# HGRN2 sample states updated by VectorE and ScalarE in half-head steps, without the GpSimd passes

## The chip, the cores and the metric

The kernel runs on one core of one Trainium2 chip, in one launch. The metric is the device time of that core in microseconds (us). Three runs of the kernel before took 1523.41, 1524.83 and 1525.97 us; the median, 1524.83 us, is the time before.

## The reference, cut to what matters

One step of a hybrid decoder layer works on 256 prompt tokens and 8 sample tokens (one new token for each of 8 running sequences). A projection of width 88 x 128 feeds a short convolution and an HGRN2 recurrence with 8 heads of 128 x 128 state; their outputs are merged by gates, projected, and followed by a squared-ReLU MLP. For a sample token the recurrence is one step of the state, and its output is a product with q:

```python
f = lb + (1.0 - lb) * sigmoid(fz)
kk = 1.0 - f
S = f[..., None] * S + kk[..., None] * v[None, :]     # per sequence and head, 128 x 128
o = q @ S
```

All sample states of the 8 heads (8 x 8 x 128 x 128 float32, 4 MB) are read, updated and written back.

## The kernel before, in words

Features lie on partitions, the 264 tokens on the free axis. Every matrix product is formed from exact halves: an operand x is split into `hi` (a rounded copy, ScalarE, line 58) and `lo` (x minus `hi`, VectorE, line 59), and each 128 x 128 weight block takes three matmuls (lines 85 to 87). So each weight chunk of 128 x 2048 (1 MB, one output tile of 128 features) asks for two casts `whi` on ScalarE, two subtractions `wlo` on VectorE, both 1024 columns wide, and 48 matmuls on TensorE.

The input projection (phase 1) is written out by hand as a list of 56 slots, `seq`. In slot i the program issues, in this order: the fetch of the weights of tile i + 2 (SyncE's queue), the evacuation of tile i - 1 from PSUM (VectorE, line 445), the casts and subtractions for tile i + 1, the work that stands in `todo` for the slot, then the 48 matmuls of tile i, then the TensorE work in `todo_pe`. Two raw weight buffers and four `whi`/`wlo` buffers (two tiles) connect the engines. Each engine works through its own queue strictly in order.

The recurrence of two heads (2j and 2j + 1) is cut into stages 0 to 14, one for each successive slot (function `hgrn`; the last lines of it list them). The stages that matter here:

- Stage 3 issues six transfers of 512 KB: for each head `so` (the state), `fb` and `qb` (f and q of the sample tokens, broadcast to all partitions).
- Stage 4: VectorE multiplies `kend`, `kin`, `qin`; GpSimd runs `s_mul(0)`: `so = so * fb`, then `fb = 1 - fb` (lines 254, 255). TensorE transposes `iv` and `kend` after the slot's matmuls (lines 298, 299).
- Stage 5: ScalarE copies `vk` (line 305); GpSimd runs `s_mul(1)`; VectorE runs `s_upd(0)`: eight times `so[:, t] = fb[:, t] * v + so[:, t]` on 128 columns (line 260). TensorE runs `sco(0)` (lines 314, 320).
- Stage 6: VectorE runs `sta(0)` (lines 325 to 329), which empties the PSUM tiles of `sco(0)`; there are three such tiles, so `sco(1)`, at the end of the slot, waits for `sta(0)`.
- Stage 7: `sta(1)`; GpSimd runs `s_out(0)`: `qb = qb * so` (line 265), and `so` is sent out. TensorE runs `ops` (lines 343, 347).
- Stages 8 to 10: `s_upd(1)`, then `s_red(0)` (a sum of `qb`, line 269) and `s_out(1)`, then `s_red(1)`.

Pair 0 has stage 4 in slot 8; pair 1 in slot 20, pair 2 in slot 32, pair 3 in slot 44. The convolution's work lies between: `conv_u` on GpSimd, `conv` one slot later (ScalarE line 409, then VectorE line 411), `conv_split` one slot after that.

Of the kernel before, what the change touches and what calls it, by code (L numbers as in the profile page):

```python
# [11 lines left out]
AF = mybir.ActivationFunctionType  # L12
ALU = mybir.AluOpType
# [3 lines left out]
TP = 256  # L17
TS = 8
# [20 lines left out]
@with_exitstack  # L39
def hybrid_step(ctx: ExitStack, tc: tile.TileContext, x, par, sconv, shg, w_hd, w_in, w_br, w_out, w_up, w_dn,  # L40
                y, nconv_p, nhg_p, nconv_s, nhg_s):
    """Feature-major throughout: features on partitions, the 256 prompt and 8 sample tokens on the free
    axis.  Every GEMM operand is split exactly into float32r parts (hi + lo), and each product is formed
    as hi*hi + hi*lo + lo*hi in float32 PSUM."""
    nc = tc.nc
    PS = bass.MemoryType.PSUM

# [20 lines left out]
        return w  # L68

    def split_w(w, h):  # L70
        """Half h of a [128, 16*128] weight chunk -> list of 8 (hi, lo) stationary tiles."""
        hi = wsp.tile([P, 8, P], F32R, tag="hi", name="whi")
        lo = wsp.tile([P, 8, P], F32R, tag="lo", name="wlo")
        split(w[:, h * 1024:(h + 1) * 1024].rearrange("p (k c) -> p k c", c=P), hi, lo)
        return [(hi[:, k], lo[:, k]) for k in range(8)]
# [16 lines left out]
    def t264(name):  # L92
        return tmp.tile([P, T], F32, tag="t", name=name)

# [1 line left out]
    ones = const.tile([P, P], F32, name="ones")  # L96
    nc.vector.memset(ones, 1.0)
    eps = const.tile([P, 1], F32, name="eps")
    nc.vector.memset(eps, EPS)
    warm = const.tile([P, 1], F32, name="warm")  # L100
# [5 lines left out]
    NB = T // 3  # L106

    def sumsq(ps, ss, start, stop):
        """Column sums of ss, tokens on partitions: ps[t, b] = sum over p of ss[p, b * NB + t]."""
        for b in range(3):  # L110
            nc.tensor.matmul(ps[:NB, b:b + 1], ss[:, b * NB:(b + 1) * NB], ones[:, 0:1],
                             start=(start and b == 0), stop=(stop and b == 2))

    def rstd_diag(ps, n, name):
        """Diagonal blocks of 1/sqrt(sum/n + eps) from the column sums in ps."""
        r = const.tile([NB, 3], F32, name="r_" + name)
        nc.vector.tensor_scalar(r, ps[:NB, 0:3], 1.0 / n, EPS, op0=ALU.mult, op1=ALU.add)
        nc.vector.reciprocal(r, r)
        nc.scalar.activation(r, r, AF.Sqrt)
        dg = const.tile([NB, 3, NB], F32, tag="dg", name="dg_" + name)  # L120
        nc.vector.tensor_tensor(dg, ident[:NB, 0:NB].unsqueeze(1).broadcast_to([NB, 3, NB]),
                                r.unsqueeze(2).broadcast_to([NB, 3, NB]), op=ALU.mult)
        return dg

    def rstd_bcast(dg, name):
        """The per-token factors of dg, on all partitions, in PSUM."""
        bps = mps.tile([P, 512], F32, tag="m", name="bps_" + name)[:, :T]
        nc.tensor.matmul(bps, ones[:NB], dg.rearrange("p b t -> p (b t)"), start=True, stop=True)
        return bps

# [1 line left out]
    pt = const.tile([P, N_PAR], F32, name="pt")  # L132
    xg = []
    ss1 = const.tile([P, T], F32, name="ss1")
# [4 lines left out]
    for g in range(4):  # L139
# [9 lines left out]
        for j in range(4):  # L149
            k = 4 * g + j  # L150
            gk = pt[:, C_NMIX + k:C_NMIX + k + 1]
            hi = act.tile([P, T], F32R, tag="xg", name=f"xgh{k}")
# [17 lines left out]
    nc.gpsimd.tensor_tensor(ss1, xsq[:, 0], xsq[:, 1], op=ALU.add)  # L170
    p0.close()

# [1 line left out]
    ident = const.tile([P, P], F32, name="ident")  # L174
    make_identity(nc, ident)
    cmask = const.tile([P, 2, P], F32, name="cmask")
# [5 lines left out]
    nc.gpsimd.memset(smask, 1.0)  # L182
    nc.gpsimd.memset(smask.rearrange("p a (n l) -> p (a n) l", l=CH)[:, :, 0:1], 0.0)

# [1 line left out]
    rstd1 = const.tile([P, T], F32, name="rstd1")  # L186
    ao = {}
    hctx = ExitStack()
# [15 lines left out]
        nc.gpsimd.memset(u[:, 0:2], 0.0)  # L204

    def hgrn(j, q, fz, iv, og):
        """HGRN2 of heads 2j, 2j+1, cut into stages that are issued beside successive GEMM tiles:
        stage -> (elementwise part, TensorE part)."""
        st = {}

        def s0():
# [37 lines left out]
                                    b3[:, :, CH - 1:CH].broadcast_to([P, 8, CH]), b3, op=ALU.subtract)  # L249
            st["b"] = b.rearrange("p (a t) -> p a t", a=2)  # L250

        def s_mul(i):
            fb, qb, so = st["s", i]
            nc.gpsimd.tensor_tensor(so, so, fb, op=ALU.mult)
            nc.gpsimd.tensor_scalar(fb, fb, -1.0, 1.0, op0=ALU.mult, op1=ALU.add)

        def s_upd(i):
            fb, qb, so = st["s", i]
            for t in range(TS):
                nc.vector.scalar_tensor_tensor(so[:, t], fb[:, t], iv[:, i, TP + t:TP + t + 1], so[:, t],  # L260
                                               op0=ALU.mult, op1=ALU.add)

        def s_out(i):
            fb, qb, so = st["s", i]
            nc.gpsimd.tensor_tensor(qb, qb, so, op=ALU.mult)
            nc.sync.dma_start(nhg_s[2 * j + i], so)

        def s_red(i):
            nc.vector.tensor_reduce(out=st["o"][:, i, TP:], in_=st["s", i][1], axis=AX.X, op=ALU.add)
# [15 lines left out]
        def s4():  # L285
            st["qin"] = pair_tile("qin", w=TP)
            nc.vector.tensor_tensor(st["kend"], st["kend"], st["kk"][:, :, :TP], op=ALU.mult)
            nc.vector.tensor_tensor(st["kin"], st["kin"], st["kk"][:, :, :TP], op=ALU.mult)
            nc.vector.tensor_tensor(st["qin"], q[:, :, :TP], st["eb"], op=ALU.mult)
            s_mul(0)  # L290

        def s4p():
            for i in range(2):
# [8 lines left out]
        def s5():  # L302
            for i in range(2):
                st["vk", i] = hp.tile([P, 4, P], F32, tag=f"vk{i}", name=f"vk{i}")
                nc.scalar.copy(st["vk", i], st["trps", i])
            s_mul(1)
            s_upd(0)

        def sco(i):
            ps = mps.tile([P, 512], F32, tag="m", name="scps")  # L310
# [12 lines left out]
        def sta(i):  # L323
# [4 lines left out]
            for n in range(1, 4):  # L328
# [2 lines left out]
                                               dl[n % 2][:, (n // 2) * P:(n // 2 + 1) * P],  # L331
                                               op0=ALU.mult, op1=ALU.add)

        def s7():
            sta(1)
            s_out(0)

        def s7p():
            for i in range(2):
# [10 lines left out]
        def s8():  # L350
            o = st["o"] = pair_tile("o")
            for i in range(2):
                nc.scalar.copy(o[:, i, :TP], st["ops", i][:, :TP])
            s_upd(1)
            for i in range(2):
                nc.sync.dma_start(nhg_p[2 * j + i], st["S", i][:, 3])

        def s9():
            s_red(0)
            s_out(1)  # L360

        def s10():
# [21 lines left out]
        def s14():  # L384
            for i in range(2):
# [3 lines left out]
                ao["o", 2 * j + i] = (hi, lo)  # L389

        return {0: (s0, None), 1: (s1, s1p), 2: (s2, None), 3: (s3, None), 4: (s4, s4p),
                5: (s5, lambda: sco(0)), 6: (lambda: sta(0), lambda: sco(1)), 7: (s7, s7p), 8: (s8, None),
                9: (s9, None), 10: (s10, s10p), 11: (s11, None), 12: (s12, None), 13: (s13, None), 14: (s14, None)}

    def conv_u(c, hc, cg):
# [22 lines left out]
        split(a, hi, lo)  # L418
        ao["a", c] = (hi, lo)

    # GEMM tiles in issue order, and the work to issue beside each of them
    cv = [(n, b + c, c) for c in range(NC_) for n, b in (("hc", HC), ("bg", BG), ("cg", CG))]
    seq = []
    for j in range(NH2):
# [42 lines left out]
    with tc.manual_schedule():  # L467
# [7 lines left out]
        for i in range(len(seq) + 1):  # L475
# [11 lines left out]
            if i == 0:  # L487
                gemm(ps, wk[i], xg, range(8))
                nc.scalar.copy(rstd1, rstd_bcast(dg1, "rstd1"))
                gemm(ps, wk[i], xg, range(8, 16))  # L490
                # lower bound: first entry of the softmax over the two rows of logits
                lbx = const.tile([P, 2, NC_], F32, name="lbx")
                lbm = const.tile([P, NC_], F32, name="lbm")
                lb = const.tile([P, NC_], F32, name="lb")
                oml = const.tile([P, NC_], F32, name="oml")
                lg = pt[:, C_LB:C_LB + 16].rearrange("p (r c) -> p r c", r=2)
                nc.vector.tensor_tensor(lbm, lg[:, 0], lg[:, 1], op=ALU.max)
                for r in range(2):
                    nc.vector.tensor_tensor(lbx[:, r], lg[:, r], lbm, op=ALU.subtract)
                nc.scalar.activation(lbx, lbx, AF.Exp)  # L500
                nc.vector.tensor_tensor(lbm, lbx[:, 0], lbx[:, 1], op=ALU.add)
                nc.vector.reciprocal(lbm, lbm)
                nc.vector.tensor_tensor(lb, lbx[:, 0], lbm, op=ALU.mult)
                nc.vector.tensor_scalar(oml, lb, -1.0, 1.0, op0=ALU.mult, op1=ALU.add)
            else:
                gemm(ps, wk.pop(i), xg)
# [10 lines left out]
        gemm(ps, load_w(w_in[REST.index(m)]), xg)  # L517
        nc.vector.tensor_tensor(out, ps, rstd1, op=ALU.mult)

# [1 line left out]
    mx = ctx.enter_context(tc.tile_pool(name="mx", bufs=32))  # L521
    x2p = ctx.enter_context(tc.tile_pool(name="x2p", bufs=1))
    raws.append(ctx.enter_context(tc.tile_pool(name="wraw2", bufs=2)))
# [20 lines left out]
        split(sg[0], hi, lo)  # L544
        mix.append((hi, lo))

# [1 line left out]
    x2, x2g = [], []  # L548
    ss2 = const.tile([P, T], F32, name="ss2")
    for m in range(NK):  # L550
# [18 lines left out]
        x2.append(t)  # L569
        x2g.append((hi, lo))  # L570

# [1 line left out]
    ss3 = const.tile([P, T], F32, name="ss3")  # L573
    rstd2 = None
    for qd in range(NQ):
# [36 lines left out]
                ps3 = mps.tile([P, 512], F32, tag="m", name="ps_rstd3")  # L612
                sumsq(ps3, ss3, True, False)

# [1 line left out]
    bps = rstd_bcast(rstd_diag(ps3, 2048, "rstd3"), "rstd3")  # L616
    bp = bps.unsqueeze(1)
    for m, n in ((0, 1), (1, 3), (4, 4), (8, 4), (12, 3)):
# [61 lines left out]
```

## Time and profile before

| | |
|---|---|
| median of three runs | 1524.83 us |
| span of the profiled execution | 1522.7 us |
| TensorE busy | 1493.1 us (98%) |
| VectorE busy | 905.4 us (59%) |
| ScalarE busy | 686.5 us (45%) |
| GpSimd busy | 128.3 us (8%) |
| mean granted TensorE clock | 0.991 |

The profile gives the span of one execution, from its first to its last instruction; its own device time is not on the page, and the median of the runs is 2.1 us above the span. Busy shares are averages over all phases. A row of the timeline gives start, length, engine, line, operation, output and inputs; a note in brackets is idle time of the engine just before, and what ended it. Matmuls are pipelined: their starts lie 0.12 us apart although each row is 0.28 us long.

### The profile page before, as it was taken

How to read it: one execution, taken by the hardware profiler on the slowest of the kernel's cores; microseconds unless marked ns; L12 is line 12 of the kernel's file. 1: busy time of each engine (PE TensorE's matmuls, PEld its weight loads, DVE VectorE, ACT ScalarE, POOL GpSimd, SP SyncE). 2: the span in 40 equal slices, each digit the busy share in tenths (PEclk: the TensorE clock that was granted, in tenths of full speed). 3: DMA queues.
4: the chain of work that ended last, by engine and by line, in shares of the span. 5: the costliest groups of instructions: out<-in, count | busy, mean ns of one | idle time of the engine just before them, and what ended most of it. 6: DMA issues, size and time to landing. Idle time of an engine off the chain costs nothing.

```text
span 1522.7 us, 28111 instructions
## 1 busy us (share of the span) xinstructions
PE 1493.1 (98%) x12182; PEld 1487.4 (98%) x12182; DVE 905.4 (59%) x1147; ACT 686.5 (45%) x884; POOL 128.3 (8%) x119
## 2 busy tenths in 40 slices
PE   6999999999999999999999999999999999999997
PEld 6999999999999999999999999999999999999996
DVE  8586867778655555556655544555445554455554
ACT  4454536364644444444454433444334443344452
POOL 5030404133100000001100000000000000000000
PEclk8999999999999999999999999999999999999998
DMA  5565656565655545455645454555455545454541
GB/s 191 185 238 197 250 170 249 194 250 189 236 180 181 184 176 190 171 204 194 213 167 187 174 188 173 187 173 193 168 192 172 191 169 191 169 191 170 190 166 58
DMA packets 47068, 285.90 MB, mean 188 GB/s; under 512 B 5424, under 2 KB 9024, under 8 KB 15712
## 3 DMA queue, kind: packets, MB, share of 16 engines
q1 hardware_dynamic: 46848, 283.97, 52.7%
q8 instruction: 95, 1.56, 0.4%
q14 instruction: 29, 0.24, 0.0%
q0 software_dynamic: 96, 0.14, 0.0%
HBM read 277.07 MB, written 7.02 MB: 187 GB/s over the span
## 4 chain that ended last, share of the span: by engine, by line
PE 92%; DVE 5%; DMA 1%; issue 1%; ACT 1%; SPq 0%; DVEq 0%; ACTq 0%
PE proj L85 10%; PE proj L86 9%; PE proj L87 9%; PE dn L85 8%; PE dn L87 8%; PE dn L86 8%; PE up L86 8%; PE up L85 8%; PE up L87 8%; PE wo L86 2%; PE wo L87 2%; PE wo L85 2%; DVE wlo L59 1%; PE hd L162 1%; DVE conv_a L411 1%
## 5 line engine op out<-in xcount | busy, mean ns | idle before, releaser
L58 ACT CAST whi<-w 128x1024 fp32r<-128x1024 f32 x488 | 511.1, 1050 | 766.6 <-PE dn L86 218.6
L59 DVE TENSOR_TENSOR wlo<-w,whi 128x1024 fp32r<-128x1024 f32 x488 | 604.2, 1248 | 355.5 <-ACT whi L58 353.6
L85 PE MATMUL proj<-xgh,whi 128*128 128x264 f32 x1344 | 385.3, 287 | 0.4 <-DVE q L445 0.4
L87 PE MATMUL proj<-xgh,wlo 128*128 128x264 f32 x1344 | 383.4, 285 | 0.0
L86 PE MATMUL proj<-xgl,whi 128*128 128x264 f32 x1344 | 382.6, 285 | 0.0
L85 PE MATMUL dn<-hh,whi 128*128 128x264 f32 x1024 | 293.0, 286 | 0.0
L87 PE MATMUL dn<-hh,wlo 128*128 128x264 f32 x1024 | 292.1, 285 | 0.0
L86 PE MATMUL dn<-hl,whi 128*128 128x264 f32 x1024 | 291.9, 285 | 0.0
L86 PE MATMUL up<-x2l,whi 128*128 128x264 f32 x1024 | 291.6, 285 | 0.0
L85 PE MATMUL up<-x2h,whi 128*128 128x264 f32 x1024 | 291.2, 284 | 0.0
L87 PE MATMUL up<-x2h,wlo 128*128 128x264 f32 x1024 | 290.2, 283 | 0.0
L85 PEld LDWEIGHTS proj<-xgh,whi 128*128 128x128 f32 x1344 | 254.9, 190 | 1.7 <-ACT whi L58 0.5
L86 PEld LDWEIGHTS proj<-xgl,whi 128*128 128x128 f32 x1344 | 254.7, 190 | 0.2
L87 PEld LDWEIGHTS proj<-xgh,wlo 128*128 128x128 f32 x1344 | 253.7, 189 | 0.0
L87 PEld LDWEIGHTS dn<-hh,wlo 128*128 128x128 f32 x1024 | 193.9, 189 | 0.0
L86 PEld LDWEIGHTS dn<-hl,whi 128*128 128x128 f32 x1024 | 193.7, 189 | 0.0
L87 PEld LDWEIGHTS up<-x2h,wlo 128*128 128x128 f32 x1024 | 193.7, 189 | 0.0
L85 PEld LDWEIGHTS dn<-hh,whi 128*128 128x128 f32 x1024 | 192.7, 188 | 0.0
L86 PEld LDWEIGHTS up<-x2l,whi 128*128 128x128 f32 x1024 | 192.5, 188 | 0.0
L85 PEld LDWEIGHTS up<-x2h,whi 128*128 128x128 f32 x1024 | 192.3, 188 | 0.0
L86 PE MATMUL wo<-mxl,whi 128*128 128x264 f32 x256 | 73.1, 286 | 0.0
L87 PE MATMUL wo<-mxh,wlo 128*128 128x264 f32 x256 | 73.1, 285 | 0.0
(392 smaller groups left out, 1384.1 us busy)
## 6 DMA issues: line engine op xcount, KB each, us to landing
w<-in_w_in_dram SPq DMA_DIRECT2D x84, 1024.0 KB, 4.8
w<-in_w_up_dram SPq DMA_DIRECT2D x64, 1024.0 KB, 4.7
w<-in_w_dn_dram SPq DMA_DIRECT2D x64, 1024.0 KB, 4.7
w<-in_w_br_dram SPq DMA_DIRECT2D x16, 1024.0 KB, 4.8
w<-in_w_out_dram SPq DMA_DIRECT2D x16, 1024.0 KB, 4.8
so<-in_shg_dram SPq DMA_DIRECT2D x8, 512.0 KB, 7.3
fb<-scr SPq DMA_DIRECT2D x8, 512.0 KB, 8.7
qb<-scr SPq DMA_DIRECT2D x8, 512.0 KB, 10.0
```

What stands on the lines that cost most here:

```text
L58: nc.scalar.copy(hi, src)
L59: nc.vector.tensor_tensor(lo, src, hi.bitcast(F32), op=ALU.subtract)
L85: nc.tensor.matmul(ps, wh, xh, start=(k == 0), stop=False)
L86: nc.tensor.matmul(ps, wh, xl, start=False, stop=False)
L87: nc.tensor.matmul(ps, wl, xh, start=False, stop=(k == n - 1))
L162: nc.tensor.matmul(hps[i], a[:, i * P:(i + 1) * P], b, start=st, stop=sp)
L411: nc.vector.scalar_tensor_tensor(dst, src[r], cw[r], dst, op0=ALU.mult, op1=ALU.add)
```

## The change

`s_mul`, the GpSimd part of the update, is gone. The update is now written f * (s - v) + v: VectorE forms (so - v) * fb on 128 columns, and ScalarE adds v to it, as an Identity activation with v as bias. The eight sample tokens of a head are handled in two groups of four: for head 0 in stages 5 and 6, for head 1 in stages 7 and 9. The product `qb * so` moves from GpSimd to VectorE, for head 0 from stage 7 to stage 8, for head 1 it stays in stage 9. The comments and docstrings that are removed too are left out here.

```diff
-        def s_mul(i):
+        def s_upd(i, ts):
+
             fb, qb, so = st["s", i]
-            nc.gpsimd.tensor_tensor(so, so, fb, op=ALU.mult)
-            nc.gpsimd.tensor_scalar(fb, fb, -1.0, 1.0, op0=ALU.mult, op1=ALU.add)
-
-        def s_upd(i):
-            fb, qb, so = st["s", i]
-            for t in range(TS):
-                nc.vector.scalar_tensor_tensor(so[:, t], fb[:, t], iv[:, i, TP + t:TP + t + 1], so[:, t],
-                                               op0=ALU.mult, op1=ALU.add)
+            for t in ts:
+                v = iv[:, i, TP + t:TP + t + 1]
+                nc.vector.scalar_tensor_tensor(so[:, t], so[:, t], v, fb[:, t], op0=ALU.subtract, op1=ALU.mult)
+                nc.scalar.activation(so[:, t], so[:, t], AF.Identity, bias=v)
 
         def s_out(i):
             fb, qb, so = st["s", i]
-            nc.gpsimd.tensor_tensor(qb, qb, so, op=ALU.mult)
+            nc.vector.tensor_tensor(qb, qb, so, op=ALU.mult)
             nc.sync.dma_start(nhg_s[2 * j + i], so)
...
             nc.vector.tensor_tensor(st["qin"], q[:, :, :TP], st["eb"], op=ALU.mult)
-            s_mul(0)
...
-            s_mul(1)
-            s_upd(0)
+            s_upd(0, range(4))
...
+        def s6():
+            sta(0)
+            s_upd(0, range(4, 8))
+
         def s7():
             sta(1)
-            s_out(0)
+            s_upd(1, range(4))
...
-            s_upd(1)
+            s_out(0)
...
             s_red(0)
+            s_upd(1, range(4, 8))
             s_out(1)
```

Two places in the order of the engines. First VectorE in stages 5 to 7 of pair 0 (slots 9 to 11): `al` belongs to the convolution, `wlo` are the weight subtractions, `scm` and `S` are `sta`, `q` and `fz` with `proj` are evacuations. Before:

```order
L260 SCALAR_TENSOR_TENSOR so<-fb,iv,so 128x128 x8
L59 TENSOR_TENSOR al<-conv_a,ah 128x264
L445 TENSOR_TENSOR q<-proj,rstd_461 128x264
L59 TENSOR_TENSOR wlo<-w,whi 128x1024 x2
L325 COPY_PREDICATED scm_465<-cmask,scps 128x256
L327 COPY S_1244<-dlps_1226 128x128
L329 SCALAR_TENSOR_TENSOR S_1244<-S_1244,eb,dlps_1227 128x128
L329 SCALAR_TENSOR_TENSOR S_1244<-S_1244,eb,dlps_1226 128x128
L329 SCALAR_TENSOR_TENSOR S_1244<-S_1244,eb,dlps_1227 128x128
L445 TENSOR_TENSOR fz<-proj,rstd_461 128x264
L59 TENSOR_TENSOR wlo<-w,whi 128x1024 x2
```

And after, the same stretch:

```order
L257 SCALAR_TENSOR_TENSOR so<-so,iv,fb 128x128 x4
L59 TENSOR_TENSOR al<-conv_a,ah 128x264
L445 TENSOR_TENSOR q<-proj,rstd_461 128x264
L59 TENSOR_TENSOR wlo<-w,whi 128x1024 x2
L320 COPY_PREDICATED scm_465<-cmask,scps 128x256
L322 COPY S_1240<-dlps_1222 128x128
L324 SCALAR_TENSOR_TENSOR S_1240<-S_1240,eb,dlps_1223 128x128
L324 SCALAR_TENSOR_TENSOR S_1240<-S_1240,eb,dlps_1222 128x128
L324 SCALAR_TENSOR_TENSOR S_1240<-S_1240,eb,dlps_1223 128x128
L257 SCALAR_TENSOR_TENSOR so<-so,iv,fb 128x128 x4
L445 TENSOR_TENSOR fz<-proj,rstd_461 128x264
L59 TENSOR_TENSOR wlo<-w,whi 128x1024 x2
```

Four of the eight updates ahead of `sta(0)` have moved behind it. Second, ScalarE in stages 5 to 8 of pair 0: `vk` are the copies of stage 5, `ah` the convolution's cast, `whi` the weight casts, `o` the copies of stage 8. Before:

```order
L305 COPY vk_1156<-trps 128x512
L305 COPY vk_1158<-trps 128x512
L58 CAST ah<-conv_a 128x264
L58 CAST whi<-w 128x1024 x6
L353 COPY o<-ops 128x256 x2
L58 CAST whi<-w 128x1024 x4
```

After:

```order
L301 COPY vk_1154<-trps 128x512
L301 COPY vk_1156<-trps 128x512
L258 ACTIVATE so<-so,iv 128x128 x4
L58 CAST ah<-conv_a 128x264
L58 CAST whi<-w 128x1024 x2
L258 ACTIVATE so<-so,iv 128x128 x4
L58 CAST whi<-w 128x1024 x2
L258 ACTIVATE so<-so,iv 128x128 x4
L58 CAST whi<-w 128x1024 x2
L352 COPY o<-ops 128x256 x2
L58 CAST whi<-w 128x1024 x2
L258 ACTIVATE so<-so,iv 128x128 x4
```

Between the weight casts of successive tiles there now stand groups of four activations, each of which reads what VectorE has just written.

## Rows read from the trace of the kernel before

**Rows 1.** The page's first line: the span of the profiled execution.

```profile
span 1522.7 us, 28111 instructions
```

**Rows 2.** Busy time by stretch: stretch, length, PE, PEld, DVE, ACT, POOL, PEclk, DMA share, GB/s.

```profile
100.00:200.00 100.00, 95.93 (x768) 94.22 (x767) 75.85 (x112) 47.92 (x59) 25.26 (x17) 0.97 0.59 208
200.00:300.00 100.00, 98.00 (x809) 97.01 (x808) 72.06 (x113) 48.23 (x61) 25.05 (x20) 1.00 0.59 209
```

**Rows 3.** Waits of PE up to 450 us: total us, times, longest.

```profile
PE trps L299 <- DVE kend L287: 3.0, 1, 3.0
...
PE scps L314 <- DVE scm L325: 2.5, 2, 1.7
```

**Rows 4.** Timeline of PE: one clean passage between tiles, then three that wait.

```profile
106.40 0.61 PE L314 MATMUL scps<-qin,kin 128*128 128x128 f32 x4
...
107.58 0.39 PE L85 MATMUL proj<-xgh,whi 128*128 128x264 f32 x1
...
113.40 0.28 PE L87 MATMUL proj<-xgh,wlo 128*128 128x264 f32 x1
...
116.52 0.39 PE L85 MATMUL proj<-xgh,whi 128*128 128x264 f32 x1
...
178.02 0.27 PE L298 MATMUL trps<-ident,iv 128*128 128x128 f32 x1
181.26 0.47 PE L299 MATMUL trps<-ident,kend 128*128 128x128 f32 x1 [2.96 <-DVE kend L287]
...
274.10 0.28 PE L87 MATMUL proj<-xgh,wlo 128*128 128x264 f32 x1
...
278.12 0.39 PE L85 MATMUL proj<-xgh,whi 128*128 128x264 f32 x1
```

**Rows 5.** Busy time by stretch, after the longest wait (columns as in rows 2).

```profile
181.26:187.26 6.00, 6.00 (x28) 6.00 (x29) 6.00 (x11) 2.96 (x4) 0.84 (x1) 0.50 0.30 104
```

**Rows 6.** Timeline of DVE, stages 3 to 6 of pairs 0 to 2.

```profile
104.81 2.35 DVE L59 TENSOR_TENSOR wlo<-w,whi 128x1024 fp32r<-128x1024 f32 x2
...
109.87 4.21 DVE L59 TENSOR_TENSOR wlo<-w,whi 128x1024 fp32r<-128x1024 f32 x2
...
171.00 3.20 DVE L411 SCALAR_TENSOR_TENSOR conv_a<-ub,pt,conv_a 128x256 f32<-128x256 f32 x2 [1.71 <-ACT conv_a L409]
...
178.38 2.83 DVE L287 TENSOR_TENSOR kend<-kend,kk 128x512 f32<-128x512 f32 x1
...
248.25 1.00 DVE L411 SCALAR_TENSOR_TENSOR conv_a<-ub,pt,conv_a 128x256 f32<-128x256 f32 x2
...
269.20 3.00 DVE L411 SCALAR_TENSOR_TENSOR conv_a<-ub,pt,conv_a 128x256 f32<-128x256 f32 x2
```

**Rows 7.** Timeline of POOL, the passes that lie beside those rows.

```profile
109.35 2.52 POOL L265 TENSOR_TENSOR qb<-qb,so 128x1024 f32<-128x1024 f32 x1 [6.46 <-DVE so L260]
...
171.50 2.41 POOL L254 TENSOR_TENSOR so<-so,fb 128x1024 f32<-128x1024 f32 x1 [5.76 <-DMA fb<-scr]
...
177.83 2.82 POOL L254 TENSOR_TENSOR so<-so,fb 128x1024 f32<-128x1024 f32 x1 [2.73 <-DMA fb<-scr]
...
269.36 2.56 POOL L265 TENSOR_TENSOR qb<-qb,so 128x1024 f32<-128x1024 f32 x1 [3.26 <-DVE so L260]
```

**Rows 8.** Instructions of lines 260 and 409: ns as min/median/max, first and last start.

```profile
L260 DVE SCALAR_TENSOR_TENSOR so<-fb,iv,so x64: 337/346/351, 107.1 to 365.9; 128x128 f32<-128x128 f32 x64
...
L409 ACT ACTIVATE conv_a<-ub,pt x8: 492/504/506, 95.0 to 394.2; 128x256 f32<-128x256 f32 x8
L409 ACT ACTIVATE conv_a<-us,pt x8: 287/288/289, 95.4 to 394.6; 128x8 f32<-128x8 f32 x8
```

**Rows 9.** Timeline of ACT: two weight casts behind their transfer.

```profile
181.47 2.00 ACT L58 CAST whi<-w 128x1024 fp32r<-128x1024 f32 x2 [5.18 <-DMA w<-in_w_in_dram]
```

**Rows 10.** Timeline of DVE: first and last row of one `sta`.

```profile
193.47 0.45 DVE L325 COPY_PREDICATED scm<-cmask,scps 128x256 f32<-128x256 uint32 x1
...
194.19 1.11 DVE L329 SCALAR_TENSOR_TENSOR S<-S,eb,dlps 128x128 f32<-128x128 f32 x3
```

More of the change, by code (lines that the diff above doesn't have):

```diff
@@ L391, in hgrn @@
         return {0: (s0, None), 1: (s1, s1p), 2: (s2, None), 3: (s3, None), 4: (s4, s4p),
-                5: (s5, lambda: sco(0)), 6: (lambda: sta(0), lambda: sco(1)), 7: (s7, s7p), 8: (s8, None),
+                5: (s5, lambda: sco(0)), 6: (s6, lambda: sco(1)), 7: (s7, s7p), 8: (s8, None),
                 9: (s9, None), 10: (s10, s10p), 11: (s11, None), 12: (s12, None), 13: (s13, None), 14: (s14, None)}
```

## The prediction

> **What bounds the kernel now.** I read the page first: a span of 1522.7 us [rows 1], in which TensorE is busy nearly all the time. A change on three other engines can then only win what TensorE loses in phase 1, so the next view is the busy time by stretch: it loses 4.07 us between 100 and 200 us and 2.00 us between 200 and 300 us, and the clock is below full in the first of these [rows 2]. The waits of TensorE name the cause: the transposes wait 3.0 us for `kend`, the scores `scps` 2.5 us for `scm`, both VectorE work of the recurrence [rows 3]. So phase 1 is bound by TensorE except at a few places where VectorE is late.
>
> The timeline of TensorE prices each place. A clean passage over `sco`, from `scps` to the next tile's first matmul, takes 107.58 - 106.40 = 1.18 us [rows 4]. The tile from 107.58 has its last matmul at 113.40, so 48 matmuls come at 5.82 / 47 = 0.124 us. Against that:
> - pair 0: from the last matmul at 113.40 to the next tile at 116.52 there are 3.12 us; less 0.12 and 1.18, 1.82 us are lost.
> - pair 1: the second transpose starts at 181.26, 3.24 us after the first, where the 0.12 of a matmul would do: 3.12 us are lost. Behind it TensorE runs for 6.00 us at a granted clock of 0.50, the lower of its two levels (1.2 GHz) [rows 5]; that is half the work, so 3.00 us more. Sum 6.12 us.
> - pair 2: 278.12 - 274.10 = 4.02 us, less 0.12 and 1.18: 2.72 us.
>
> Together 10.66 us. That is the most this part of the program can give back, apart from fractions.
>
> Why is VectorE late there? The rows of VectorE and of GpSimd lie side by side. Two `wlo` take 2.35 us at 104.81 and 4.21 us at 109.87; GpSimd's pass starts at 109.35 [rows 6, 7]. The two convolution steps take 1.00 us at 248.25, but 3.20 us at 171.00 and 3.00 us at 269.20, with GpSimd passes from 171.50 and 269.36; `kend` takes 2.83 us beside the pass from 177.83. In each case the VectorE instruction ends about when the pass does. So the passes are cheap on their own engine and dear on VectorE's.
>
> **The change part by part.** *GpSimd's passes go.* What they cost VectorE at the three places: pair 0, 4.21 - 2.35 = 1.86 us. Pair 1, 3.20 - 1.00 = 2.20 us, and on `kend` at least 2.83 - 1.18 = 1.65 us (a product of 512 columns can't cost more than one of 1024, half of the 2.35 us pair); sum at least 3.85 us. Pair 2, 3.00 - 1.00 = 2.00 us. What remains on GpSimd (the convolution's products) still lies beside VectorE, and stays.
>
> *VectorE's own work.* The 64 updates of 0.346 us [rows 8] stay 64 updates of the same shape. Ahead of `sta(0)` there are four fewer, at most 4 x 0.346 = 1.4 us; rows of one engine overlap a little at their ends, so I take 1.1. The product `qb * so` comes to VectorE, 8 x 1.18 = 9.4 us by half the `wlo` pair; from below 8 x 0.346 x 2, since 1024 columns can't be cheaper than two updates of 128, from above 8 x 2.1 (half of the contended pair, though its cause is then gone). I take 9.4. It falls in stages 8 and 9. Stage 8 has evacuation and `wlo` (2.7 us) and this product, under 4 us of the 5.9 us that a slot of 48 matmuls lasts; it loses eight updates. Stage 9 has 2.7 us, the reduction (1024 columns again, 1.2), four updates and the product, some 6.4 us: late by half a microsecond, which stage 10, with one reduction, takes back. So on the path: nothing.
>
> *ScalarE's 64 Identity activations.* No ScalarE row of 128 columns is on record. With scale or bias from a tile, 8 columns take 0.288 us and 256 take 0.504 us [rows 8], so the cost lies between these; by columns it is 0.39 us, which I take. In total 25 us, in a stretch where ScalarE is busy less than half the time [rows 2]. What matters is the queue: each group of four waits for VectorE, and the weight casts of the next tile stand behind it, on which the next `wlo` wait. This makes a ring: two casts of 1.00 us [rows 9] with the pair of `wlo` starting after the first, 1.00 + 2.35; then `sta`, from 193.47 to 194.19 + 1.11, 1.83 us [rows 10]; then four updates, 1.38; then the last activation, 0.39. Sum 6.95 us from one group to the next. TensorE's slot is 48 x 0.124 + 1.18 = 7.1 us in stages 5 and 6, and longer in stage 7. The ring fits, with 0.15 us to spare; so its price is 0. With 0.288 us an activation it is 6.85; with 0.504 it is paced by ScalarE, 3.35 + 1.83 + 0.35 + 4 x 0.504 = 7.54 us, 0.44 us too long, twice a pair: 0.9 us a pair if no slack stood ahead of it, 3.5 us over four pairs. The cover of both ends is the tile of lead that the four weight buffers give.
>
> The Trainium skill speaks against putting this addition there: ScalarE: Activation LUTs, section Rules for kernel authors, sends additions to VectorE and budgets about 0.3 us for an activation with a pointer bias plus 0.83 ns an element. By it an estimate for 128 columns is 0.41 us, the ring 3.35 + 1.83 + 0.35 + 1.62 = 7.15 us, and the sum would change by 0.1 us a slot at most; no row before shows the shape itself, and the two measured shapes lie on either side.
>
> *New waits.* The first update now waits on VectorE for `so` and `fb`, where GpSimd waited before. In pair 1 GpSimd could start at 171.50 and 177.83 [rows 7], so both heads' data had landed then, and VectorE comes to them only behind the `wlo` of the weights that land at 181.47 [rows 9]; nothing. Those weights themselves land no earlier than before; they are needed one tile later. On SyncE's queue the output of head 0's state moves behind one more weight fetch, which helps, and that of head 1 now waits for ScalarE's last activation, with the next fetch queued behind; its weights are cast two slots later, which covers the 3 us.
>
> In pair 2 the convolution falls in stage 5, behind the four activations on ScalarE; VectorE waits there for line 409, whose two pieces (0.504 and 0.288) start when the activations are through: about 1.0 us.
>
> **The sum.** Pair 0: VectorE is earlier by 1.86 + 1.1 = 2.96 us against 1.82 lost; all of it comes back. Pair 1: earlier by 3.85 against a wait of 3.12; the wait goes, and with it the low clock: 6.12. Pair 2: 2.00 + 1.1 - 1.0 = 2.1 of 2.72. Sum 10.04 us. For small new waits, above all in stage 10, where TensorE needs a square that comes after the late reduction, I take off 0.2 us a pair, an estimate: 9.24 us. The profiled execution of 1522.7 us becomes 1513.5; the runs' median lies 2.1 us above that span, so the time is 1515.6 us.
>
> **Rivals.**
> 1. *Only the short waits go.* Should something else be late where `kend` was (weights that land just then, as in rows 9, and the casts behind them), the low clock returns too. For it: the transfers of stage 3 and the weights compete in this stretch. Against: the wait names `kend`, not weights. Then 1.82 + 2.1 and perhaps half of 6.12 make up to 7 us less, or none of it 3.9: 1518 to 1521, say 1520.
> 2. *VectorE gets no freer.* The product costs it 9.4 us, and passes between would be made up by slack anyway. For it: 76 of 100 us busy in the first stretch of rows 2. Against: the product falls in stages 8 and 9, the waits in 4 to 6. Time: 1524.8, within noise.
> 3. *The ring is too slow: slower than before.* If each activation waits for its own update and pays 0.3 us for the handover on top of 0.504, the group takes 3.2 us and the ring 3.35 + 1.83 + 0.35 + 3.2 = 8.7 us, 1.6 over in stages 5 and 6 and 0.6 in stage 7: 3.8 us a pair, 15 in all, and twice 3 us of low clock. Less the 10 us won, 1536 at worst; where the handover is smaller, near 1529. It decides from about 2.5 us lost a pair, a ring of 8.2 us. Against: whichever end of the durations I take, the ring stays below 7.6.
>
> **How the numbers follow.** The forecast case, 1513 to 1517.5, has 0.60; rival 1 has 0.20; rival 2 has 0.11; rival 3 has 0.09. A measurement tells no change from changes over 0.2%, 3.0 us. Faster takes the forecast, rival 1 and 0.03 of rival 2: 0.83. Same takes the rest of rival 2 and a little of rival 3: 0.09. Slower has 0.08. The range reaches down to 1511.5 (all 10.66 us, fractions elsewhere, and runs that spread by 2.5 us) and up to 1521.5, which holds rival 1.
>
> **What would show it.** Right: TensorE busy in 99 or more of 100 us from 100 to 300 us, no clock of 0.50 near 180, convolution pairs near 1.0 us and `kend` near 0.7 us on VectorE, `qb` products near 1.2 us. The activations should take 0.3 to 0.5 us and start within 0.2 us of their update's end. Wrong: TensorE waiting for `whi` or `wlo` in stages 6 to 10, activations that alternate with updates at 0.7 us or more, a new wait for `scm` in all four pairs, or `sq` late at stage 10.

## The result, and the profile after

The changed kernel takes 1514.79 us (median of four runs, 1514.25 to 1515.34) against 1524.67 us for the kernel before; the ratio is 0.9937 with a 95% interval of 0.9923 to 0.9951. In a second comparison on another occasion (e9 below) it was 0.9927, 0.9915 to 0.9939. So the change makes the kernel 9.9 us, or 0.6%, faster. Forecast were 1515.6 us, and a range of 1511.5 to 1521.5.

The page's first lines, after: the span, and busy time of each engine with its share and instructions. They answer to [rows 1].

```profile
span 1513.6 us, 28155 instructions
## 1 busy us (share of the span) xinstructions
PE 1488.3 (98%) x12182; PEld 1483.0 (98%) x12182; DVE 895.6 (59%) x1155; ACT 703.2 (46%) x948; POOL 77.3 (5%) x95
```

GpSimd has lost 51 us. VectorE has taken over eight products and is still 10 us less busy than before. Busy time by stretch, after, in the columns of [rows 2], and all waits of TensorE that are left between 38 and 430 us, as in [rows 3]:

```profile
100.00:200.00 100.00, 100.00 (x834) 98.89 (x833) 72.41 (x122) 57.84 (x91) 7.44 (x8) 1.00 0.61 217
200.00:300.00 100.00, 100.00 (x826) 99.24 (x825) 72.33 (x109) 56.48 (x85) 9.75 (x13) 1.00 0.60 216
```

```profile
PE proj L85 <- DVE q L445: 0.4, 1, 0.4
PE onps L370 <- ACT sq L365: 0.2, 1, 0.2
```

TensorE is busy all the time, at full clock; the waits for `kend` and `scm` are gone. Its timeline at the three places of [rows 4]: pair 0's passage over `sco(1)`, pair 1's transposes, pair 2's passage.

```profile
113.75 0.61 PE L309 MATMUL scps<-qin,kin 128*128 128x128 f32 x4
...
114.94 0.39 PE L85 MATMUL proj<-xgh,whi 128*128 128x264 f32 x1
...
176.43 0.27 PE L294 MATMUL trps<-ident,iv 128*128 128x128 f32 x1
176.53 0.27 PE L295 MATMUL trps<-ident,kend 128*128 128x128 f32 x1
...
266.69 0.61 PE L309 MATMUL scps<-qin,kin 128*128 128x128 f32 x4
...
267.87 0.39 PE L85 MATMUL proj<-xgh,whi 128*128 128x264 f32 x1
```

The passages take 1.19 and 1.18 us, the clean value, and the second transpose follows the first by 0.10 us. Why is seen on VectorE; these rows answer to [rows 6]:

```profile
109.25 2.36 DVE L59 TENSOR_TENSOR wlo<-w,whi 128x1024 fp32r<-128x1024 f32 x2 [0.17 <-ACT whi L58]
...
169.40 1.01 DVE L411 SCALAR_TENSOR_TENSOR conv_a<-ub,pt,conv_a 128x256 f32<-128x256 f32 x2 [1.71 <-ACT conv_a L409]
...
173.80 0.69 DVE L284 TENSOR_TENSOR kend<-kend,kk 128x512 f32<-128x512 f32 x1
...
260.90 1.00 DVE L411 SCALAR_TENSOR_TENSOR conv_a<-ub,pt,conv_a 128x256 f32<-128x256 f32 x2 [0.96 <-ACT conv_a L409]
```

Where 4.21, 3.20, 2.83 and 3.00 us stood, there are 2.36, 1.01, 0.69 and 1.00 us.

Where the time went shows at the start of the merge phase, at its first matmul (`br0a`); before, then after, in the view of an instruction's first and last start:

```profile
L85 PE MATMUL br0a<-ah,whi x8: 280/284/287, 410.6 to 413.2; 128*128 128x264 f32 x8
```

```profile
L85 PE MATMUL br0a<-ah,whi x8: 279/285/286, 400.3 to 402.9; 128*128 128x264 f32 x8
```

Phase 1 gave 10.3 us. The span gained only 9.1: the last part, from TensorE's last product to the end, cost 1.2 us more in this execution. Nearly half of that is one matmul pair at the lower clock (granted 1.00 before, 0.50 after): the broadcast of the final norm, in the kernel before and after.

```profile
1513.23 0.69 PE L128 MATMUL bps_rstd<-dg_rstd,ones 88*128 88x264 f32 x2 [1.25 <-DVE dg_rstd L121]
```

```profile
1502.94 1.22 PE L128 MATMUL bps_rstd<-dg_rstd,ones 88*128 88x264 f32 x2 [1.24 <-DVE dg_rstd L121]
```

### The profile page after: what moved, and what is told of

Read it like the earlier page. It is cut to its first block, busy times and chain, and to the rows that moved or that the text cites. A ratio compares the mean times of both kernels' runs of the same rounds, so it can differ in the third digit from the quotient of the medians.

```text
span 1513.6 us, 28155 instructions
## 1 busy us (share of the span) xinstructions
PE 1488.3 (98%) x12182; PEld 1483.0 (98%) x12182; DVE 895.6 (59%) x1155; ACT 703.2 (46%) x948; POOL 77.3 (5%) x95
## 4 chain that ended last, share of the span: by engine, by line
PE 96%; DVE 1%; DMA 1%; issue 0%; ACT 0%; SPq 0%; DVEq 0%; ACTq 0%
PE proj L85 11%; PE proj L86 10%; PE proj L87 10%; PE dn L85 8%; PE dn L87 8%; PE up L85 8%; PE dn L86 8%; PE up L86 8%; PE up L87 8%; PE wo L86 2%; PE wo L87 2%; PE wo L85 2%; DMA w<-in_w_hd_dram 1%; PE hd L162 1%; PE dlps L315 0%
## 5 line engine op out<-in xcount | busy, mean ns | idle before, releaser
L59 DVE TENSOR_TENSOR wlo<-w,whi 128x1024 fp32r<-128x1024 f32 x488 | 597.7, 1234 | 376.0 <-ACT whi L58 374.1
```

The costliest lines, as they stand in the source:

```text
L59: nc.vector.tensor_tensor(lo, src, hi.bitcast(F32), op=ALU.subtract)
```

## The experiments

Theory 1: GpSimd's passes read the state while VectorE works, hold VectorE's two-input instructions up, and so make `kend` and `scm` late. Theory 2: the gain comes from the half-head steps, with four updates fewer ahead of `sta(0)`. Beside these two stood the question what the new ring between ScalarE and VectorE costs. All times are medians; each comparison has its own runs of the kernel before (1524.06 us for e1 to e4, 1524.54 for e5 to e7, 1526.19 for e8 and e9).

**e1: only the product moves.** The kernel before, with one line of it changed:

```diff
-            nc.gpsimd.tensor_tensor(qb, qb, so, op=ALU.mult)
+            nc.vector.tensor_tensor(qb, qb, so, op=ALU.mult)
```

> The kernel before with one edit: the product qb * so on VectorE instead of GpSimd (stages 7 and 9); s_mul stays on GpSimd. Theory 1 (GpSimd passes held VectorE up): the product lay beside wlo in pair 0 and beside the convolution in pair 2, so the two waits for scm shrink (1.8 of 1.8 us and about 2.0 of 2.7 us), the wait of pair 1 for kend and the 6 us of low clock stay: 1520 to 1521.5 us. Theory 2 (the gain comes from the half-head steps, four updates fewer ahead of sta(0)): no step is changed here, VectorE has 9.4 us more to do: 1524.5 us or more.

Measured: 1519.38 us (1516.68 to 1521.90), ratio 0.9966, 0.9953 to 0.9979, 0.6 us below theory 1's range. TensorE's waits between 38 and 430 us, and its clock behind the wait of pair 1:

```profile
PE trps L299 <- DVE kend L287: 4.0, 2, 3.0
PE proj L85 <- DVE q L445: 0.4, 1, 0.4
PE dlps L320 <- DVE S L329: 0.3, 1, 0.3
```

```profile
177.80:183.80 6.00, 5.98 (x50) 5.99 (x51) 6.00 (x11) 3.91 (x5) 0.87 (x1) 1.00 0.24 97
```

The waits for `scm` are gone and the 3.0 us for `kend` stay, as theory 1 says. Theory 2 falls: no step was changed. Two things were not expected. Pair 3 now waits for `kend` too, 1.0 us, because there the pass of `s_mul(1)` falls beside `kend`. And the clock did not fall behind the wait of 3.0 us: 1.00, where it was 0.50 before [rows 5].

**e2: the passes of `s_mul` put back** into the changed kernel, `s_old(0)` in stage 4 and `s_old(1)` in stage 5 (the two calls are left out below):

```diff
+        def s_old(i):
+            fb, qb, so = st["s", i]
+            old = hp.tile([P, TS, P], mybir.dt.bfloat16, tag="old", name="old")
+            nc.gpsimd.tensor_tensor(old, so, fb, op=ALU.mult)
+            nc.gpsimd.tensor_scalar(old, fb, -1.0, 1.0, op0=ALU.mult, op1=ALU.add)
```

> The kernel after, with the two GpSimd passes of s_mul put back at their old places (stages 4 and 5), reading so and fb and writing a scratch tile (bfloat16, for want of room) that nobody reads. Theory 1: nothing waits for them, but they lie beside VectorE's convolution and kend in pair 1 again; the wait of about 3 us for kend and the 6 us at the lower clock return, and the short waits don't: 1519.5 to 1521.5 us. Theory 2: the passes cost nothing, 1514.8 us within 1.

Measured: 1520.71 us (1517.51 to 1522.27), ratio 0.9975, 0.9964 to 0.9986. In its profile TensorE waits for `kend` again, and VectorE is held as before; the waits, then VectorE and GpSimd in pair 1, then the six microseconds after the wait.

```profile
PE trps L302 <- DVE kend L290: 3.9, 2, 2.9
```

```profile
169.34 3.18 DVE L419 SCALAR_TENSOR_TENSOR conv_a<-ub,pt,conv_a 128x256 f32<-128x256 f32 x2 [1.71 <-ACT conv_a L417]
...
176.70 2.83 DVE L290 TENSOR_TENSOR kend<-kend,kk 128x512 f32<-128x512 f32 x1
```

```profile
169.84 2.40 POOL L255 TENSOR_TENSOR old<-so,fb 128x1024 bf16<-128x1024 f32 x1 [5.76 <-DMA fb<-scr]
...
175.96 3.02 POOL L255 TENSOR_TENSOR old<-so,fb 128x1024 bf16<-128x1024 f32 x1 [2.53 <-DMA fb<-scr]
```

```profile
179.58:185.58 6.00, 6.00 (x37) 6.00 (x38) 5.99 (x10) 3.71 (x7) 0.85 (x1) 0.72 0.28 104
```

Nobody uses the passes' results, and they bring the wait back: theory 1 again. (The second wait for `kend`, 1.0 us, is pair 3's, as in e1.) The clock behind it was 0.72 on average here: the lower level held for only a part of the stretch.

**e8: GpSimd as busy, but not reading.** As e2, with another body; the first line only sets the start.

```diff
-            nc.gpsimd.tensor_tensor(old, so, fb, op=ALU.mult)
-            nc.gpsimd.tensor_scalar(old, fb, -1.0, 1.0, op0=ALU.mult, op1=ALU.add)
+            nc.gpsimd.tensor_tensor(old[:, 0, 0:1], so[:, 0, 0:1], fb[:, 0, 0:1], op=ALU.mult)
+            for _ in range(4):
+                nc.gpsimd.memset(old, 0.0)
```

> The kernel after, with GpSimd busy at the places of the old passes but not reading: per head a product of one element of so and fb (so that it starts when they have landed), then four memsets of a 128x1024 bfloat16 scratch tile that nobody reads, some 2 to 4 us. Reading theory (a VectorE instruction with two inputs in SBUF is held while GpSimd reads SBUF): memsets read nothing, convolution and kend keep their 1.0 and 0.7 us, no wait for kend: 1514.8 us within 1. Activity theory (any GpSimd instruction holds VectorE up): the wait for kend returns, 1519 to 1522 us, as with the passes put back.

Measured: 1513.67 us (1512.94 to 1515.04), ratio 0.9925, 0.9912 to 0.9939, no different from the changed kernel. GpSimd in pairs 1 and 3, then VectorE beside it:

```profile
168.97 3.98 POOL L257 MEMSET old<- 128x1024 bf16 x4
...
326.58 3.98 POOL L257 MEMSET old<- 128x1024 bf16 x4
```

```profile
170.36 2.35 DVE L59 TENSOR_TENSOR wlo<-w,whi 128x1024 fp32r<-128x1024 f32 x2
...
326.99 1.00 DVE L420 SCALAR_TENSOR_TENSOR conv_a<-ub,pt,conv_a 128x256 f32<-128x256 f32 x2
```

In pair 1 the pair of `wlo` lies wholly beside the memsets and takes its clean 2.35 us; in pair 3 the convolution's two steps do, and take their clean 1.00 us. (In pair 1 the convolution ran ahead of the memsets, and `kend` lay beside them for 0.4 us at most; for `kend` this run shows little.) So it is not GpSimd's activity that holds VectorE up but its reading. The Trainium skill says the same (SBUF — State Buffer, section Who interferes with whom): a VectorE instruction with two inputs in SBUF contends with a GpSimd instruction that reads SBUF, not with one that only writes. The traces agree: the convolution's two steps took 3.18 us beside reads (e2, pair 1) and 1.00 us beside writes (here, pair 3).

**e3: only the product back on GpSimd**, in the changed kernel, in stages 8 and 9:

```diff
-            nc.vector.tensor_tensor(qb, qb, so, op=ALU.mult)
+            nc.gpsimd.tensor_tensor(qb, qb, so, op=ALU.mult)
```

> The kernel after, with only the product qb * so on GpSimd again (now in stages 8 and 9). Theory 1: a pass is dear only where VectorE is late, and stages 8 and 9 have slack; 1514.8 us within 1. If each removed pass is worth its share of the gain, about a third of 9.9 us is lost: 1517 to 1518.5 us.

Measured: 1517.42 us (1517.21 to 1518.45), ratio 0.9958, 0.9945 to 0.9970. That is a miss: 2.6 us above the changed kernel's 1514.79, not within 1. It lies in the range of the other view, that each pass is worth its share; where TensorE waits says otherwise. TensorE's longest waits, then GpSimd's product and VectorE in stages 9 and 10 of pair 1:

```profile
PE onps L370 <- ACT sq L365: 2.3, 4, 1.0
PE ops L342 <- DVE scm L320: 0.6, 1, 0.6
```

```profile
210.47 2.40 POOL L262 TENSOR_TENSOR qb<-qb,so 128x1024 f32<-128x1024 f32 x1 [17.58 <-ACT so L258]
```

```profile
211.36 3.73 DVE L59 TENSOR_TENSOR wlo<-w,whi 128x1024 fp32r<-128x1024 f32 x2
215.02 1.21 DVE L266 TENSOR_REDUCE o<-qb 128x8 f32<-128x1024 f32 x1
```

The pass holds the `wlo` of stage 10 (3.73 instead of 2.35 us), the reduction behind them comes late, then the square, and TensorE waits for it in all four pairs. Stage 10 has no slack: the changed kernel already waits there once.

**e4: whole heads.** The changed kernel with `s_upd(0, range(8))` in stage 5, `s_out(0)` in stage 7, `s_upd(1, range(8))` in stage 8, `s_out(1)` in stage 9:

```diff
-            s_upd(0, range(4))
+            s_upd(0, range(8))
...
-            s_upd(0, range(4, 8))
...
-            s_upd(1, range(4))
+            s_out(0)
...
-            s_out(0)
+            s_upd(1, range(8))
...
-            s_upd(1, range(4, 8))
```

> The kernel after, with the update in whole heads at the old places: eight updates of head 0 in stage 5, eight of head 1 in stage 8, products in stages 7 and 9, all without GpSimd. Theory 1: no pass beside VectorE, so pair 1 keeps its gain; eight updates and activations ahead of the next casts put sta(0) off by 1.2 us, which costs up to 1.1 us in pair 2 and little elsewhere: 1515 to 1517 us. Theory 2: the short waits of pairs 0 and 2 return in full, 1.8 + 2.7 us: about 1519.3 us.

Measured: 1516.18 us (1515.08 to 1516.87), ratio 0.9946, 0.9934 to 0.9959. TensorE waits 0.3 us for `scm` and 0.3 for `S`, in pair 2. By the medians the halves are worth 1.4 us of the 9.9, which the two intervals, as they overlap, do not tell from nothing; theory 2's 1519.3 falls.

**e5 and e6: the ring loaded.** One more activation, and three more, behind each of the 64:

```diff
                 nc.scalar.activation(so[:, t], so[:, t], AF.Identity, bias=v)
+                for _ in range(1):      # e6: range(3)
+                    nc.scalar.activation(junk, fb[:, t], AF.Identity, bias=v)
```

> The kernel after, with one more Identity activation of 128 columns behind each of the 64, into a scratch tile that nobody reads: 25 us more of ScalarE by duration, about 19 us by distance. Ring theory (activation, casts, wlo, sta, updates, activation paces stages 5 to 7; 6.95 us of a slot's 7.1): a group is 1.2 us longer, the ring 8.1 us, so scps waits about 0.3 to 1.1 us in stage 6 and ops about 1 us in stage 7 of each pair, and the square of stage 10 is 1.2 us later: 1.5 to 3 us a pair, 1520 to 1526 us. Slack theory (ScalarE is busy only 60% of the stretch, so it takes this in its idle time): 1514.8 us within 1.

> As with one more activation, but three more behind each of the 64: a group is 3.6 us longer. Ring theory: 10.5 us against 7.1, 3.4 us late in each of stages 6 and 7 and at stage 10, 8 to 10 us a pair, and waits long enough that the granted clock falls to 0.50 for some microseconds in some pairs: 1545 to 1570 us. Slack theory (57 us of distance into some 120 us of idle ScalarE time): 1514.8 to 1518 us.

Measured: e5 1523.17 us (1521.46 to 1525.13), ratio 0.9992, 0.9983 to 1.0001; e6 1584.78 us (1583.16 to 1586.69), ratio 1.0400, 1.0385 to 1.0414. The groups of stages 5 to 7 in pair 0 of the changed kernel:

```profile
106.68 1.28 ACT L258 ACTIVATE so<-so,iv 128x128 f32<-128x128 f32 x4 [0.77 <-DVE so L257]
...
113.66 1.28 ACT L258 ACTIVATE so<-so,iv 128x128 f32<-128x128 f32 x4 [3.50 <-DVE so L257]
...
120.32 1.28 ACT L258 ACTIVATE so<-so,iv 128x128 f32<-128x128 f32 x4 [3.48 <-DVE so L257]
```

The first activations of the same groups in e5, then in e6, then TensorE's longest waits in e6:

```profile
105.73 0.40 ACT L259 ACTIVATE so<-so,iv 128x128 f32<-128x128 f32 x1 [0.77 <-DVE so L258]
...
113.89 0.40 ACT L259 ACTIVATE so<-so,iv 128x128 f32<-128x128 f32 x1 [3.49 <-DVE so L258]
...
121.73 0.41 ACT L259 ACTIVATE so<-so,iv 128x128 f32<-128x128 f32 x1 [3.48 <-DVE so L258]
```

```profile
105.06 0.40 ACT L259 ACTIVATE so<-so,iv 128x128 f32<-128x128 f32 x1 [0.77 <-DVE so L258]
...
116.72 0.40 ACT L259 ACTIVATE so<-so,iv 128x128 f32<-128x128 f32 x1 [3.50 <-DVE so L258]
```

```profile
PE onps L373 <- ACT sq L368: 17.1, 3, 5.7
PE scps L312 <- DVE scm L323: 11.1, 4, 3.4
PE ops L345 <- DVE scm L323: 4.9, 4, 1.8
```

The ring is 6.98 and 6.66 us in the changed kernel (6.95 was worked out), 8.16 and 7.84 us in e5 (8.1), 11.66 us in e6 (10.5 was expected). e5 falls into its range, but not by the way that was expected for it. Its longest waits of TensorE between 38 and 430 us (beside 0.4 us for `q`, as in the changed kernel):

```profile
PE onps L373 <- ACT sq L368: 3.9, 4, 2.4
PE dlps L318 <- DVE S L327: 0.6, 2, 0.3
```

The waits forecast for `scps` in stage 6 and `ops` in stage 7 are not there, though the ring is longer than a slot. The square of stage 10 is late in all four pairs: in pair 0 VectorE's product waits 1.45 us for the activations of stage 9, 0.56 us in the changed kernel, and the reduction and the square stand behind it. Counted by the starts of the tiles, against the changed kernel, stage 10 costs 4.6 us in the four pairs and stages 6 and 7 cost 2.1 us, all of it in pairs 2 and 3. So idle time of ScalarE does not hide the added activations, but most of what they cost is lost at stage 10. e6 is above its range. Its ring is longer than I took, since the three activations into one scratch tile put the next one off by 1.16 us, 0.39 each, not 0.30; and its mean clock from 100 to 400 us was 0.93, lower levels in every pair, where I had expected some.

**e7: the addition on VectorE**, in the changed kernel:

```diff
-                nc.scalar.activation(so[:, t], so[:, t], AF.Identity, bias=v)
+                nc.vector.tensor_scalar(so[:, t], so[:, t], v, None, op0=ALU.add)
```

> The kernel after, with the addition of v on VectorE (a tensor_scalar on 128 columns) instead of ScalarE. Ring theory: the ring loses its ScalarE leg (the casts no longer stand behind the activations), VectorE gets 64 instructions of 0.2 to 0.35 us; four of them put stage 6 off by about 1 us while the casts come 1 us earlier. TensorE waits for nothing either way: 1514 to 1516 us. If VectorE is the engine that is short in these stages, each pair loses about 1 us at scps: 1518 to 1519 us.

Measured: 1517.05 us (1515.42 to 1519.13), ratio 0.9955, 0.9942 to 0.9967: a miss by one microsecond, but not at `scps` either. TensorE's longest wait, and the two engines' instructions (e7, then the changed kernel):

```profile
PE onps L370 <- ACT sq L365: 2.0, 4, 0.9
```

```profile
L258 DVE TENSOR_SCALAR so<-so,iv x64: 286/286/291, 106.8 to 368.0; 128x128 f32<-128x128 f32 x64
```

```profile
L258 ACT ACTIVATE so<-so,iv x64: 384/387/404, 106.7 to 364.1; 128x128 f32<-128x128 f32 x64
```

The addition is cheaper on VectorE, 0.286 against 0.387 us, and the kernel is slower with it: stage 9 becomes longer, and stage 10's square is late in all four pairs, as in e3.

**e9: the changed kernel again**, unedited.

> The changed kernel itself, so that the experiments have it beside them on a chip: 1514 to 1516 us, with runs that lie within 1.5 us of each other, since it has no wait after which the clock may fall.

Measured: 1514.13 us, but 1513.20 to 1515.86, 2.7 us apart and not 1.5. The kernel before spread from 1522.47 to 1526.47 in the same comparison. The two profiled executions of the changed kernel, with spans of 1513.6 and 1511.5 us, hardly differ in phase 1: from the first matmul of the slots to `br0a` it took 354.0 us (from 46.3) and 353.9 us (from 44.8), and before 364.5 us (from 46.1). Their 2.1 us lie at the start and the end of the program.

No experiment points to a version faster than the changed kernel: what TensorE still waits in phase 1 is 0.6 us.

## Why the prediction was right

*The bound.* TensorE's losses in phase 1 were the whole prize: the forecast sum was 10.04 us, or 9.24 with 0.8 taken off for small new waits, and phase 1 gave 10.3.

*The passes.* The clean durations worked out for VectorE came as forecast: 2.36, 1.01 and 1.00 us; for `kend` I had used 1.18 as a bound, it is 0.69. That a VectorE instruction ends about when the pass does was read a little wrong: the convolution and `kend` end 0.3 to 0.6 us later, and the `wlo` pair of pair 0 ended 2.2 us after its pass (114.08 and 111.87). It stands until the pass ends, and what is left of its own work comes after that. That contention was the cause is shown by e1, e2 and e8, each with one part alone. By parts: without the product's pass alone 1519.38; with the passes of `s_mul` alone 1520.71; without any, in whole heads, 1516.18; with halves, 1514.79.

*The low clock.* Here a term was right only for the execution it was read from. Pair 1's wait was priced at 3.12 us and 3.00 us more for the clock. The same wait of 3 us went with 0.50 for six microseconds before, a mean of 0.72 in e2, and 1.00 in e1. Counted by the starts of the tiles, against the changed kernel, the wait and what follows it cost 5.9 us before, 4.8 in e2 and 3.2 in e1. So the wait is in every run of these kernels that was profiled, and the price of the clock is not. The runs fit loosely: with this wait they spread over 4.0 to 5.2 us (the kernel before beside the experiments, e1, e2; but 2.6 us in the four runs of the kernel before that the result rests on), without it over 1.1 to 2.7 us (after, e3, e4, e8, e9), though e5 and e7 spread over 3.7 without it. The runs' mean clocks go with their times, in e1 from 0.995 in the fastest to 0.992 in the slowest; but so they do in e7, from 0.995 to 0.991. So the clock has a part in the spread; how much of it comes from this wait was not tested.

*Pair 2.* I let 0.6 us remain, since the convolution waits for ScalarE. It does wait, 0.96 us at 260.90, and yet nothing remained. I had not counted that the `wlo` pair of stage 5 was held too, by the second pass of `s_mul(1)`; VectorE and GpSimd before, then VectorE after:

```profile
263.96 3.21 DVE L59 TENSOR_TENSOR wlo<-w,whi 128x1024 fp32r<-128x1024 f32 x2 [2.18 <-ACT whi L58]
```

```profile
264.06 2.04 POOL L255 TENSOR_SCALAR fb<-fb 128x1024 f32<-128x1024 f32 x1
```

```profile
256.54 2.36 DVE L59 TENSOR_TENSOR wlo<-w,whi 128x1024 fp32r<-128x1024 f32 x2 [3.02 <-ACT whi L58]
```

That gave 0.85 us more.

*The ring.* 6.95 us was the estimate and 6.98 and 6.66 the measure; the activation, taken at 0.39 us between 0.288 and 0.504, is 0.387. That 6.98 comes so near is in part luck: it contains the convolution's cast `ah`, which I had left out and which puts the weight casts off by 0.30 us; 6.66 is the ring without it. And that it fits only just is not shown: e5's rings of 8.16 and 7.84 us are longer than the slot of 7.1 us in stages 5 and 6, and in pairs 0 and 1 they cost TensorE nothing in stages 6 and 7, so the tile of lead covers more than I gave it. e5 stands at rival 3's point of decision, 8.2 us, and takes as long as the kernel before, but it loses most of that at stage 10, which rival 3 did not name. e6's 11.66 us do cost waits for `scm`, up to 3.4 us.

*Stage 10.* I took off 0.2 us a pair for the late square. It was 0.2 us in one pair. But that the place is so narrow came out only in e3 and e7, whose expectations missed for that reason: I had credited stages 8 to 10 with slack that stage 10 doesn't have.

*The remainder.* The estimate of 2.1 us between span and median holds loosely: 1513.6 against 1514.79. Each run's time lies 1.65 to 1.77 us above its own span; the rest is which run was profiled. That the forecast comes within 0.8 us is partly luck: phase 1 gave 1.1 us more than the 9.24 counted, and the end of the program took 1.2 back.

## What to carry to other kernels

When an engine off the critical path looks nearly idle, compare the durations of the same instruction beside its work and away from it: GpSimd was 8% busy, and the four passes of [rows 7] stretched VectorE's instructions to between 1.8 and 4 times their length. Price what such a pass does at the places where the bounding engine waits, not by its own length; elsewhere it costs nothing (before, GpSimd was busy for 30 us between 300 and 400 us, and TensorE for all 100). Before moving work to an engine with idle time, close the ring: add up what the moved step waits for and what waits behind it, and compare with the period of the engine that bounds. Then look for the next thing that this engine needs behind the ring: in e3, e5 and e7 the time was lost there, at stage 10.

## What the runs showed of the hardware

Four GpSimd memsets of 1024 columns (3.98 us) ran beside two-input VectorE instructions without lengthening them (2.35 us for the `wlo` pair, 1.00 us for the convolution's). Beside GpSimd's products such instructions stood until the product ended: `kend`, 0.69 us long elsewhere and begun at 178.38, ended 0.56 us after the product that ran to 180.65. A scaling, which reads one input, held the `wlo` pair from 263.96 in the same way (3.21 us). A wait of 2.95 to 3.00 us on TensorE was followed by a granted clock of 0.50, 0.72 or 1.00 over the next six microseconds in three kernels that hardly differ there.
